# Feed-forward of a two-layer encoder trunk: the linear half scaled after w_down, more pairs by seven products

## The chip, the cores and the metric

The kernel runs on one core of one Trainium2 chip. The metric is the device time of one execution in microseconds (us): the median of the runs, and beside it the time and the span of one profiled execution. In rows of the profile, PE is the matmul engine (TensorE), PEld its weight loads, DVE is VectorE, ACT is ScalarE, POOL is GpSimd and SP the queue that issues most transfers.

## What is computed

Two layers over T = 528 tokens (16 meta tokens and 512 frames) of D = 1024. In each layer a mixer with two branches, and then a feed-forward with a short causal convolution on its gate; D_FF is 2816:

```python
def conv_gated_mlp(n, w_up, conv_w, w_down):
    gate, up = jnp.split(n @ w_up, 2, axis=-1)
    gate = causal_dwconv(gate, conv_w)          # three taps
    return (jax.nn.silu(gate) * up) @ w_down

    n = rms_norm(h, norm_ffn[l])
    h = h + conv_gated_mlp(n, w_up[l], conv_ffn[l], w_down[l])
```

`rms_norm` multiplies each token by a number of its own (`rb` in the kernel) and each feature by a gain. `rb` is the same for all features of a token, so it can be multiplied in on either side of a matmul that sums over features. On the way to `gate` it must stand ahead of silu; on `up`, which enters linearly, it can also stand behind `w_down`.

## The kernel before

Activations lie with features on the 128 partitions and tokens along the free axis. All operands are float32; each is split into a high and a low part (`wh`, `wl` of a weight tile, index 0 and 1 of an activation), and a product is three matmuls: high x high, high x low, low x high. A matmul takes 128 x 128 weights and up to 512 tokens into one PSUM bank. There are eight banks, two for each of the tags "a", "g", "s" and "x".

Weights come by `stage` (a load on SP into one of four `wst` buffers) and `two` (ScalarE copies the high part, VectorE subtracts for the low part, into one of three `wh` and three `wl` buffers). `tc.high_priority(HI)` puts these ahead of other work. A scheduler writes the order of each engine's queue when the kernel is built, by priority (program order otherwise) and by its own costs. On the chip each engine runs its queue in that order, and waits by semaphores.

In layer 0 all 528 tokens are worked on, in two halves of 264. In layer 1 only what is needed for the 512 frames: the gate in halves of about 257, the up half in one piece of 512 (one bank).

The feed-forward (`ffn`) first runs over FT = 22 columns j of the up-projection. A plain column has two calls of `dense` (the matmuls of L268): gate into tag "g" or "a", up into "s" or "a", for j even or odd. The gate is multiplied by `rb` into `cs` (L1133), convolved (L1136, L1138), and gated by tanh (L1140, L1141); the up half leaves its banks by a product with `rb` (L1148) and is multiplied by the gated half (L1149). For j in UP, gate and up come together from `up7`, by `seven` (matmuls at L284): a 2 x 2 block scheme with seven products for eight (the up half is then multiplied by `rb` at L1143), over pairs of k tiles, two output tiles and two token halves. Its banks are X1, X2 (tag "x"), two of tag "g" or "a", and `b2` of tag "s". The order in `seven` is: products into X1 and C0, then C2 (T4), then X2 and X1 (T2, T1), then C1 and X2 (B22, T3), with `steps` of additions between. Sums of weight blocks (L302 to L305) and of activation blocks are its operands; those for w_up are made after w_out in `layer`, in `xar` and `xq`. At j = 0, the statistics of the norm and the broadcast `rb` (`nf.stats`, `nf.rows`, L205 and L220 to L223) come among the matmuls: gate, statistics, the up half `pu0`, `rbp`, `rb`.

Then come four pairs m0 of output tiles of w_down. The last 2 x SP of the 22 k tiles go by `strassen` (`seven` over J0 to FT; its X1 is copied to P1 and combined to U2, U3, U4), the others by plain matmuls (`others`, L1245). For the first pair `strassen` stands ahead of the last piece of `others`, for the later ones ahead of all. Results are added to `hk`, which holds the residual stream (L1211, `addto`; L1263 where `wide`, that is, both halves in one bank, in layer 1 up to m0 = 4). After each pair of layer 0 the next norm is fed (`feed`: L187, L188, L194, L195); in layer 1 the tiles go to the output.

Of the kernel before, what the change touches and what calls it, by code (L numbers as in the profile page):

```python
# [10 lines left out]
F32 = mybir.dt.float32  # L11
# [16 lines left out]
SP = 4  # L28
INV = -2e38
UP = (2, 5, 8, 11, 14)  # L30
# [84 lines left out]
def _trunk(es, tc, nc, a):  # L115
# [162 lines left out]
    def seven(src, ks, ops, sums, X1, X2, C0, C1, C2, first, steps):  # L278
# [7 lines left out]

        def run(jobs, w, i, stride, off):

            for o, res, name, blk in jobs:
                for q in range(2):  # L290
                    mm3(o, first(res) if i == 0 and q == 0 else False, w, off * blk + stride * q, ops[2 * i + q][name])
# [6 lines left out]
        for i, r in enumerate(raw):  # L298
            t12, t34 = [t.rearrange("p (a q c) -> p a q c", a=2, q=2) for t in sums(i)]
            A = [r[i // 2][:, :, 128 * (i % 2):128 * (i % 2) + 128] for i in range(4)]  # L300
# [5 lines left out]
            ss.append([t.rearrange("p a q c -> p (a q c)") for t in (t12, t34)])  # L306
        n = range(len(ks))
        for i in n:
            run([(X1, "X1", "B11", 0), (C0, 0, "B21", 1)], wa[i], i, 256, 128)
        steps[0]()  # L310
        for i in n:
            w = [t.rearrange("p q c -> p (q c)") for t in two(raw[i][1][:, :, 128:], 256)]
            run([(C2, 2, "T4", 0)], w, i, 128, 0)
        for i in n:
            run([(X2, "X2", "T2", 1), (X1, "X1", "T1", 0)], two(ss[i][0], 512), i, 128, 256)
        steps[1]()
        for i in n:
            run([(C1, 1, "B22", 1), (X2, None, "T3", 0)], two(ss[i][1], 512), i, 128, 256)
# [6 lines left out]
    def layer(l, nm, before=None):  # L325
# [683 lines left out]
        for m in range(8):  # L1009
# [3 lines left out]
            if m % 2 == 0:  # L1013
                yt = Q((2, 3, 8, 9)[m // 2], [128, 2, 2, T], F32R, name="Y")
# [14 lines left out]
        xq = None  # L1029
        nf.ops = []  # L1030
        for m0 in range(0, 8, 2):
# [17 lines left out]
            if i == 3:  # L1049
                xq = Q(10, [128, 2112], F32R, name="xq")  # L1050
            tv = (xq if i == 3 else xar[:, 8 * nh * i:])[:, :8 * nh].rearrange("p (a b t) -> p a b t", a=4, b=2)
# [20 lines left out]
    def ffn(l, nf, h1, t0):  # L1072
# [11 lines left out]

        def up7(j, cs, uu):
# [23 lines left out]
            seven([a["w_up"][l, 2 * j + u] for u in range(2)], (0, 4), nf.ops,  # L1109
# [3 lines left out]
        for j in range(FT):  # L1113
            if j == J0:
                far = p1.tile([128, AR], F32R, tag="ar", name="far")
# [11 lines left out]
            if j in UP:  # L1127
                uu = p2.tile([128, T], F32, tag="hk", name="uu", bufs=2)
                up7(j, cs, uu)
                V.tensor_tensor(cs[:, 2 + t0:2 + T], cs[:, 2 + t0:2 + T], rb[:, t0:], op=mul)  # L1130
# [10 lines left out]
            V.scalar_tensor_tensor(cv[:, t0:], th[:, t0:], 1.0, cv[:, t0:], op0=add, op1=mul)  # L1141
            if j in UP:
                V.tensor_tensor(uu[:, t1:], uu[:, t1:], rb[:, t1:], op=mul)  # L1143
            else:
                ps = pu0 if j == 0 else dense(a["w_up"][l, 2 * j + 1], KT, lambda k, part: X[k][:, part], t1, "sa"[j % 2])
                uu = p2.tile([128, T], F32, tag="hk", name="uu", bufs=2)
                for p, t in ps:
                    V.tensor_tensor(uu[:, t], p, rb[:, t], op=mul)  # L1148
            V.tensor_tensor(uu[:, t1:], uu[:, t1:], cv[:, t1:], op=mul)  # L1149
            if j >= J0:  # L1150

                ys = yt[:, :8 * nh].rearrange("p (a b t) -> p a b t", a=4, b=2)
                ye = far[:, 6 * nh * ((j - J0) // 2):6 * nh * ((j - J0) // 2 + 1)].rearrange("p (a b t) -> p a b t", a=3, b=2)
# [12 lines left out]
                else:  # L1166
# [3 lines left out]
                    parts(ye[:, 0:2], halves(ue))  # L1170
                    V.tensor_tensor(uu[:, s1], uu[:, s1], ue[:, s1], op=sub)
                    parts(ye[:, 2:3], uu[:, None, s1])
                    S7.append(dict(B11=ys[:, 0], B21=ys[:, 1], B22=ys[:, 2], T1=ys[:, 3], T2=ye[:, 0], T3=ye[:, 1], T4=ye[:, 2]))
# [13 lines left out]
        for m0 in range(0, 8, 2):  # L1187
# [21 lines left out]
            def addto(i, x):  # L1209
                d = hks[i // 2][:, (s1, s2)[i % 2]]  # L1210
# [139 lines left out]
```

## Time and profile before

| what | value |
|---|---|
| median of 3 runs | 1697.04 us (1694.74 to 1697.94) |
| the profiled execution | 1696.78 us |
| its span, first to last instruction | 1695.0 us |
| granted TensorE clock, mean | 0.998 of full speed |
| TensorE busy | 1682.9 us, 99% |
| VectorE busy | 1360.1 us, 80% |
| ScalarE busy | 819.0 us, 48% |
| feed-forward of layer 0 (from the first gate matmul) | 479.64 to 858.45 us of the span |
| feed-forward of layer 1 | 1325.60 to 1691.60 us |

Matmuls are pipelined, so the duration of a record (some 284 ns for 264 columns) is not what one costs; the distance from start to start, or the length of a piece of the chain divided by its matmuls, is. Instructions on VectorE that follow each other without a wait overlap by some 0.08 us. Times in the rows count from the start of the span.

### The profile page before, as it was taken

The page shows a single profiled execution, that of the slowest core. Times are in us where ns is not written, and L with a number is a line of the kernel's source. Part 1 is how long each engine was busy: PE and PEld are TensorE (multiplying, and loading weights), DVE is VectorE, ACT ScalarE, POOL GpSimd, SP SyncE. Part 2 cuts the span into 40 slices and gives each one's busy share as a digit, 9 for nine tenths or more (in the row PEclk, how much of TensorE's full clock was granted, in tenths as well). Part 3 has the DMA queues.
Part 4 walks back from the last instruction along what each step waited for, and adds up shares of the span by engine and source line. Part 5 has one row for each costly group of instructions (what it writes and reads, how often), then busy time and mean ns, then how long its engine had stood idle before and what let it go on. Part 6 is the DMA issues. An engine that isn't in the chain of part 4 may idle for free.

```text
span 1695.0 us, 35229 instructions
## 1 busy us (share of the span) xinstructions
PE 1682.9 (99%) x13476; PEld 1579.7 (93%) x13476; DVE 1360.1 (80%) x3229; ACT 819.0 (48%) x1779; POOL 75.8 (4%) x190
## 2 busy tenths in 40 slices
PE   9999999999999999999999999999999999999999
PEld 8899988889999999999998999888899999999888
DVE  7899899866788888766558998998767888887754
ACT  6553556553444444434335534566635544444432
POOL 1000111100000000000100000110000000000000
PEclk9999999999999999999999999999999999999999
DMA  6322211225533333234433222112255433333443
GB/s 209 98 64 88 76 46 51 73 75 174 174 121 95 99 94 94 88 104 145 156 103 99 63 88 82 52 45 76 70 176 174 125 94 94 95 98 94 127 123 100
DMA packets 95097, 173.81 MB, mean 103 GB/s; under 512 B 10704, under 2 KB 15536, under 8 KB 94672
## 3 DMA queue, kind: packets, MB, share of 16 engines
q1 hardware_dynamic: 93456, 167.01, 32.5%
q10 hardware_dynamic: 1472, 4.54, 0.7%
q8 instruction: 106, 1.74, 0.4%
q14 instruction: 63, 0.52, 0.1%
HBM read 154.04 MB, written 17.06 MB: 101 GB/s over the span
## 4 chain that ended last, share of the span: by engine, by line
PE 90%; DVE 6%; ACT 3%; issue 1%; DMA 0%; ACTq 0%; DVEq 0%
PE a L268 55%; PE a L284 10%; PE a L1245 9%; PE misc L347 2%; PE iq L347 2%; PE vps L784 2%; PE oBT L947 1%; PE isc L530 1%; PE tps L795 1%; DVE wl L243 1%; PE logit L923 1%; PE PTp L941 1%; PE dS L838 1%; ACT ar L833 0%; ACT wh L242 0%
## 5 line engine op out<-in xcount | busy, mean ns | idle before, releaser
L268 PE MATMUL a<-X,wh 128*128 128x264 f32 (+4 forms) x4208 | 837.1, 295 | 0.6 <-DVE cs L1133 0.6
L268 PEld LDWEIGHTS a<-X,wh 128*128 128x128 f32 x4208 | 666.9, 189 | 17.7 <-issue 1.4
L268 PE MATMUL a<-X,wl 128*128 128x264 f32 (+4 forms) x2104 | 618.4, 294 | 0.0
L242 ACT ACTIVATE wh<-wst 128x512 fp32r<-128x512 f32 (+2 forms) x512 | 309.5, 605 | 537.7 <-PE a L268 284.6
L243 DVE TENSOR_TENSOR wl<-wst,wh 128x512 fp32r<-128x512 f32 (+2 forms) x512 | 335.8, 656 | 153.3 <-ACT wh L242 138.3
L268 PEld LDWEIGHTS a<-X,wl 128*128 128x128 f32 x2104 | 397.9, 189 | 9.1
L1245 PE MATMUL a<-F,wh 128*128 128x264 f32 (+2 forms) x728 | 154.8, 309 | 0.0
L1245 PEld LDWEIGHTS a<-F,wh 128*128 128x128 f32 x728 | 118.0, 188 | 7.3
L1245 PE MATMUL a<-F,wl 128*128 128x264 f32 (+2 forms) x364 | 112.7, 310 | 0.0
L268 PE MATMUL a<-Y,wh 128*128 128x264 f32 (+2 forms) x512 | 92.9, 283 | 0.0
L268 PEld LDWEIGHTS a<-Y,wh 128*128 128x128 f32 x512 | 79.1, 188 | 0.0
L268 PE MATMUL a<-Y,wl 128*128 128x264 f32 (+2 forms) x256 | 72.5, 283 | 0.0
L1245 PEld LDWEIGHTS a<-F,wl 128*128 128x128 f32 x364 | 68.6, 188 | 3.8
L1138 DVE SCALAR_TENSOR_TENSOR cv<-cs,vec,cv 128x528 f32<-128x528 f32 (+1 forms) x88 | 66.7, 758 | 2.7 <-ACT cv L1136 2.1
L405 DVE SCALAR_TENSOR_TENSOR cv<-cs,vec,cv 128x528 f32<-128x528 f32 x72 | 54.4, 758 | 0.9 <-ACT cv L403 0.8
L888 DVE MAX8 m<-ar 128x8 f32<-128x256 f32 (+2 forms) x96 | 53.2, 554 | 1.1
L889 DVE MATCH_REPLACE8 ar<-m,ar 128x256 f32<-128x256 f32 (+2 forms) x96 | 51.9, 541 | 0.0
L268 PEld LDWEIGHTS a<-Y,wl 128*128 128x128 f32 x256 | 48.2, 188 | 0.0
L284 PE MATMUL a<-F,wh 128*128 128x264 f32 (+1 forms) x256 | 47.9, 284 | 0.0
L284 PE MATMUL a<-xar,wh 128*128 128x264 f32 (+1 forms) x240 | 45.6, 283 | 0.0
L1140 ACT ACTIVATE th<-cv 128x528 f32<-128x528 f32 (+1 forms) x44 | 28.1, 638 | 35.7 <-DVE cv L1138 35.6
L284 PE MATMUL a<-X,wh 128*128 128x264 f32 (+1 forms) x240 | 44.8, 283 | 0.0
(401 smaller groups left out, 3057.1 us busy)
## 6 DMA issues: line engine op xcount, KB each, us to landing
wst<-w_up SPq DMA_DIRECT2D x176, 256.0 KB, 2.7
wst<-w_down SPq DMA_DIRECT2D x80, 256.0 KB, 2.7
wst<-w_a SPq DMA_DIRECT2D x64, 256.0 KB, 2.7
wst<-w_gate SPq DMA_DIRECT2D x64, 256.0 KB, 2.9
wst<-w_out SPq DMA_DIRECT2D x32, 256.0 KB, 2.9
hk<-h SPq DMA_DIRECT2D x24, 264.0 KB, 3.5
tg<-gg SPq DMA_DIRECT2D x16, 264.0 KB, 2.2
gr<-tg SPq DMA_DIRECT2D x16, 264.0 KB, 2.7
```

What stands on the lines that cost most here:

```text
L242: S.activation(h, w, AF.Copy)
L243: V.tensor_tensor(lo, w, h.bitcast(F32), op=sub)
L268: mms.append(PE.matmul(ps[j][:, :t.stop - t.start], w[:, ws], x[:, t], start=(kk == 0 and w is h and part == 0), stop=(kk == kts - 1 and w ...
L284: PE.matmul(o, ww[:, c:c + 128], x[:, part], start=st, stop=False, skip_group_check=True)
L347: mms.append(PE.matmul(b[:, c:], X[kk][:, part, o:o + 128], w[:, c:], start=(kk == 0 and w is h and part == 0), stop=(kk == KT - 1 and w i ...
L405: V.scalar_tensor_tensor(cv, cs[:, i:i + T], vc(cw + i), cv, op0=mul, op1=add)
L784: PE.matmul(p[r, ch], Ml[r, ch], U[r, ch], start=True, stop=True)
L888: V.max(m8, sc)
L889: V.match_replace(sc, m8, sc, SEL)
L1138: V.scalar_tensor_tensor(cv[:, t0:], cs[:, t0 + i:i + T], vec[:, cw + i:cw + i + 1], cv[:, t0:], op0=mul, op1=add)
L1140: S.activation(th[:, t0:], cv[:, t0:], AF.Tanh, scale=0.5)
L1245: PE.matmul(o, ww[:, 128 * k:128 * k + 128], Yf[k0 + k][:, part, t], start=first(2 * u + h) if k == 0 and part == 0 and ww is w[0] else False,
```

## The change

It has five parts.

1. UP has six columns, (1, 3, 6, 8, 10, 13), for five, (2, 5, 8, 11, 14).
2. SP is 5 for 4: ten of the 22 k tiles of w_down go by seven products, so `seven` takes groups of 2, 2 and 1 pairs instead of 2 and 2. It stages the third group's weights when the first two have been combined.
3. The up half is no longer multiplied by `rb`; it leaves its banks by a product with the gated half `cv`. Instead, the result of w_down is multiplied by `rb` before it is added to `hk`.
4. So the partial results `us` of `strassen` are no longer added to `hk` on their own: they are added to the banks C at the end of the pair, scaled, and added to `hk`. The last pair of layer 1 (`tail`) adds its scaled `us` earlier and scales each bank by itself.
5. Operands have other places: Y in buffers 2, 3, 5, 6 (2, 3, 8, 9 before), the sums for w_up in `ar`, 8 and 10, those for w_down in free parts of `ar` and, for the fifth pair, in the buffers of X6 and X7, and the third weight sum in the buffer of `ikT`.

The diff, cut to its core:

```diff
-SP = 4
+SP = 5
-UP = (2, 5, 8, 11, 14)
+UP = (1, 3, 6, 8, 10, 13)
...
         raw, ss, wa = [], [], []
-        for k in ks:
-            r = [stage(src[u][:, k * 128:k * 128 + 512], 512).rearrange("p (q c) -> p q c", q=2) for u in range(2)]
-            raw.append(r)
-            wa.append(two(r[0].rearrange("p q c -> p (q c)"), 512))
...
+        top = [load(i, 0) for i in range(2)]
+        raw = [[top[i], load(i, 1)] for i in range(2)]
         n = range(len(ks))
+        for i in range(2):
+            wa.append(two(raw[i][0].rearrange("p q c -> p (q c)"), 256 * np_[i]))
+        for i in n:
+            if i == 2:
+                raw.append([load(2, 0), load(2, 1)])
+                wa.append(two(raw[2][0].rearrange("p q c -> p (q c)"), 256 * np_[2]))
+            combine(i)
         for i in n:
             run([(X1, "X1", "B11", 0), (C0, 0, "B21", 1)], wa[i], i, 256, 128)
         steps[0]()
         for i in n:
-            w = [t.rearrange("p q c -> p (q c)") for t in two(raw[i][1][:, :, 128:], 256)]
+            w = [t.rearrange("p q c -> p (q c)") for t in two(raw[i][1][:, :, 128:], 128 * np_[i])]
             run([(C2, 2, "T4", 0)], w, i, 128, 0)
...
-                yt = Q((2, 3, 8, 9)[m // 2], [128, 2, 2, T], F32R, name="Y")
+                yt = Q((2, 3, 5, 6)[m // 2], [128, 2, 2, T], F32R, name="Y")
...
+            xt = xar[:, 2112 * i:] if i < 2 else Q((8, 10)[i - 2], [128, 2112], F32R, name="xq")
...
+        def extra(p):
+
+            v = lambda t, n: t[:, :2 * n * nh].rearrange("p (a b t) -> p a b t", a=n, b=2)
+            if p == 4:
+                x6, x7 = [p1.tile([128, 2 * T], F32R, tag=f"X{k}", name=f"FX{k}") for k in (6, 7)]
+                return v(x6, 2), v(x7, 1)
+            o, e = ((4224, 5280), (0, 1056), (1584, 2640), (3168, 5808))[p]
+            return v(far[:, o:], 2), v(far[:, e:], 1)
...
             if j in UP:
-                V.tensor_tensor(uu[:, t1:], uu[:, t1:], rb[:, t1:], op=mul)
+                V.tensor_tensor(uu[:, t1:], uu[:, t1:], cv[:, t1:], op=mul)
             else:
                 ps = pu0 if j == 0 else dense(a["w_up"][l, 2 * j + 1], KT, lambda k, part: X[k][:, part], t1, "sa"[j % 2])
                 uu = p2.tile([128, T], F32, tag="hk", name="uu", bufs=2)
                 for p, t in ps:
-                    V.tensor_tensor(uu[:, t], p, rb[:, t], op=mul)
-            V.tensor_tensor(uu[:, t1:], uu[:, t1:], cv[:, t1:], op=mul)
+                    V.tensor_tensor(uu[:, t], p, cv[:, t], op=mul)
...
                 def sums(i):
+                    if i == 2:
+                        t = p1.tile([128, 1024], F32, tag="ikT", name="s5")
+                        return t[:, :512], t[:, 512:]
...
             us = strassen()
+            tail = last and m0 == 6
             for i, k0 in enumerate(ks[n:]):
-                if i == 1 or m0 == 0:
-                    for c, x in enumerate(us):
-                        addto(c, x)
+                if tail and i == 1:
+                    for hk, w in zip(hks, us):
+                        V.tensor_tensor(w, w, rb[:, t1:], op=mul)
+                        V.scalar_tensor_tensor(hk[:, t1:], w, 0.5, hk[:, t1:], op0=mul, op1=add)
                 others(k0)
             for u in range(2):
-                hk, m = hks[u], m0 + u
-                if wide:
-                    V.scalar_tensor_tensor(hk[:, t1:], cb[u][:, :2 * nh], 0.5, hk[:, t1:], op0=mul, op1=add)
+                hk, m, w = hks[u], m0 + u, us[u]
+                if tail:
+                    for h, t in enumerate((s1, s2)):
+                        x = w[:, nh * h:nh * h + nh]
+                        V.tensor_tensor(x, C[2 * u + h], rb[:, t], op=mul)
+                        V.scalar_tensor_tensor(hk[:, t], x, 0.5, hk[:, t], op0=mul, op1=add)
                 else:
-                    for h in range(2):
-                        addto(2 * u + h, C[2 * u + h])
+                    if wide:
+                        V.tensor_tensor(w, w, cb[u][:, :2 * nh], op=add)
+                    else:
+                        for h in range(2):
+                            x = w[:, nh * h:nh * h + nh]
+                            V.tensor_tensor(x, x, C[2 * u + h], op=add)
+                    V.tensor_tensor(w, w, rb[:, t1:], op=mul)
+                    V.scalar_tensor_tensor(hk[:, t1:], w, 0.5, hk[:, t1:], op0=mul, op1=add)
```

## Rows read from the trace of the kernel before

**Rows 1.** The page, part 1: busy us of each engine, its share of the span, and the number of its instructions.

```profile
PE 1682.9 (99%) x13476; PEld 1579.7 (93%) x13476; DVE 1360.1 (80%) x3229; ACT 819.0 (48%) x1779; POOL 75.8 (4%) x190
```

**Rows 2.** Busy time in stretches of the span: first the length in us, then the busy us of each engine with its instructions, the granted clock, the share of the transfer engines and GB/s. The first stretch is three columns of the up-projection of layer 0 (two plain, one in UP), the others are the down-projections of layer 0 and 1.

```profile
515.94:549.68 33.74, 33.74 (x279) 33.74 (x278) 29.27 (x57) 15.93 (x27) 0.30 (x3) 1.00 0.32 95
733.10:858.45 125.35, 124.29 (x1010) 123.27 (x1010) 76.94 (x163) 46.53 (x86) 4.99 (x9) 1.00 0.44 133
1572.50:1691.60 119.10, 118.95 (x757) 107.19 (x755) 68.75 (x143) 38.76 (x69) 0.00 (x0) 1.00 0.40 117
```

**Rows 3.** The chain of waits in order of time, in both feed-forwards: start, length in us, what, and how many instructions were merged. L268 are plain products of w_up (192 of 264 columns are two columns j of layer 0; 72 are one of layer 1), L284 products in `seven`, L1245 plain products of w_down (264 columns at 733.10, 512 at 1642.05, 256 at 1671.62).

```profile
515.94 23.49 PE a L268 x192
...
539.43 10.24 PE a L284 x84
...
733.10 17.54 PE a L1245 x144
...
1339.34 11.34 PE a L268 x72
...
1383.88 10.09 PE a L284 x84
...
1632.02 10.02 PE a L284 x84
1642.05 19.56 PE a L1245 x84
...
1671.62 19.95 PE a L1245 x168
```

**Rows 4.** Groups of VectorE instructions in the first stretch of rows 2, shapes apart: line, operation, out<-in, shapes, count | busy us, mean ns of one | idle us before them, and who ended it.

```profile
L243 DVE TENSOR_TENSOR wl<-wst,wh 128x512 fp32r<-128x512 f32 x10 | 6.9, 687 | 1.1 <-ACT wh L242 1.1
L1138 DVE SCALAR_TENSOR_TENSOR cv<-cs,vec,cv 128x528 f32<-128x528 f32 x6 | 4.6, 762 | 0.0
...
L1149 DVE TENSOR_TENSOR uu<-uu,cv 128x528 f32<-128x528 f32 x3 | 2.1, 702 | 0.0
L1133 DVE TENSOR_TENSOR cs<-a,rb 128x264 f32<-128x264 f32 x4 | 1.7, 431 | 1.0 <-PE a L268 1.0
```

**Rows 5.** The timeline of TensorE in layer 1, in column j = 3, which follows a UP column: start, length, what, count and, in brackets, idle time before it and who ended it.

```profile
1366.26 0.28 PE L268 MATMUL a<-X,wl 128*128 128x258 f32 x1
1366.75 0.47 PE L268 MATMUL a<-X,wh 128*128 128x512 f32 x1 [0.22 <-DVE cs L1133]
```

**Rows 6.** The chain of waits at the same place.

```profile
1365.06 0.60 DVE uu L1143
...
1366.27 0.35 DVE cs L1133
```

**Rows 7.** The chain of waits at j = 0 of layer 0: the up half `pu0`, then `rbp`.

```profile
486.65 5.94 PE a L268 x48
492.59 1.11 PE rbp L220 x10
```

**Rows 8.** The timeline of ScalarE there.

```profile
493.51 0.51 ACT L222 ACTIVATE rb<-rbp 128x400 f32<-128x400 f32 x1 [0.34 <-PE rbp L220]
493.92 0.27 ACT L223 ACTIVATE rb<-rbp 128x128 f32<-128x128 f32 x1
496.02 0.74 ACT L1136 ACTIVATE cv<-cs,vec 128x528 f32<-128x528 f32 x1 [1.83 <-DVE cs L1133]
...
498.88 0.64 ACT L1140 ACTIVATE th<-cv 128x528 f32<-128x528 f32 x1 [1.60 <-DVE cv L1138]
```

**Rows 9.** The timeline of VectorE there; the first row is the two halves of `pu0` leaving their banks.

```profile
495.84 0.76 DVE L1148 TENSOR_TENSOR uu<-a,rb 128x264 f32<-128x264 f32 x2
496.80 0.77 DVE L1138 SCALAR_TENSOR_TENSOR cv<-cs,vec,cv 128x528 f32<-128x528 f32 x1 [0.19 <-ACT cv L1136]
...
498.08 0.76 DVE L1138 SCALAR_TENSOR_TENSOR cv<-cs,vec,cv 128x528 f32<-128x528 f32 x1
...
499.56 0.71 DVE L1141 SCALAR_TENSOR_TENSOR cv<-th,cv 128x528 f32<-128x528 f32 x1 [0.37 <-ACT th L1140]
```

**Rows 10.** The timeline of TensorE in layer 0, in `seven` of the third output pair of w_down, where the products of the first T2/T1 weight tile begin. Of the two matmuls in the first row the second starts at 800.07.

```profile
799.95 0.40 PE L284 MATMUL a<-far,wh 128*128 128x264 f32 x2
800.68 0.39 PE L284 MATMUL a<-far,wl 128*128 128x264 f32 x1 [0.33 <-DVE wl L243]
```

**Rows 11.** The timeline of ScalarE there: the feed of the next norm, the high part of that tile, and the copy of X1 to P1.

```profile
798.22 0.72 ACT L187 ACTIVATE X<-hk,gains 128x528 fp32r<-128x528 f32 x1
798.85 0.62 ACT L242 ACTIVATE wh<-s 128x512 fp32r<-128x512 f32 x1
...
800.95 0.36 ACT L1219 ACTIVATE ts<-a 128x264 f32<-128x264 f32 x1
```

**Rows 12.** The timeline of VectorE there: L195 reads the square that held a "th" buffer; the last row is three low parts of weight sums, one after the other.

```profile
798.64 0.70 DVE L195 TENSOR_TENSOR sqacc<-sqacc,sqt 128x528 f32<-128x528 f32 x1
799.26 0.76 DVE L188 SCALAR_TENSOR_TENSOR X<-hk,gains,X 128x528 fp32r<-128x528 f32 x1
799.94 1.91 DVE L243 TENSOR_TENSOR wl<-s,wh 128x512 fp32r<-128x512 f32 x3
```

**Rows 13.** The end of the chain of waits.

```profile
1688.96 2.62 PE a L1245 x22
...
1691.60 0.42 DVE hk L1211
```

**Rows 14.** The chain of waits just ahead of the hand-over of rows 10, on VectorE's side.

```profile
790.67 2.68 DMA wst<-w_down
```

More of the change, by code (lines that the diff above doesn't have):

```diff
@@ L285, in mm3, with load, combine @@
                 st = False
+        base, np_ = [0], []
+        for k, n in ks:
+            np_.append(n)
+            base.append(base[-1] + n)
         def run(jobs, w, i, stride, off):
             for o, res, name, blk in jobs:
-                for q in range(2):
-                    mm3(o, first(res) if i == 0 and q == 0 else False, w, off * blk + stride * q, ops[2 * i + q][name])
+                for q in range(np_[i]):
+                    mm3(o, first(res) if i == 0 and q == 0 else False, w, off * blk + stride * q, ops[base[i] + q][name])
         raw, ss, wa = [], [], []
-        for k in ks:
-            r = [stage(src[u][:, k * 128:k * 128 + 512], 512).rearrange("p (q c) -> p q c", q=2) for u in range(2)]
-            raw.append(r)
-            wa.append(two(r[0].rearrange("p q c -> p (q c)"), 512))
-        for i, r in enumerate(raw):
-            t12, t34 = [t.rearrange("p (a q c) -> p a q c", a=2, q=2) for t in sums(i)]
-            A = [r[i // 2][:, :, 128 * (i % 2):128 * (i % 2) + 128] for i in range(4)]
+        def load(i, u):
+            k, n = ks[i]
+            return stage(src[u][:, k * 128:k * 128 + 256 * n], 256 * n).rearrange("p (q c) -> p q c", q=n)
+        def combine(i):
+            r = raw[i]
+            t12, t34 = [t[:, :256 * np_[i]].rearrange("p (a q c) -> p a q c", a=2, q=np_[i]) for t in sums(i)]
+            A = [r[b // 2][:, :, 128 * (b % 2):128 * (b % 2) + 128] for b in range(4)]
             with tc.high_priority(HI):
@@ L1083, in ffn @@
         J0 = FT - 2 * SP
+        far = nf.ar
+        def extra(p):
[5 more added lines that the diff above has]
+            return v(far[:, o:], 2), v(far[:, e:], 1)
         def up7(j, cs, uu):
@@ L1107, in end @@
                 V.tensor_tensor(uu[:, z2], X1, U3, op=add)
-            seven([a["w_up"][l, 2 * j + u] for u in range(2)], (0, 4), nf.ops,
+            seven([a["w_up"][l, 2 * j + u] for u in range(2)], ((0, 2), (4, 2)), nf.ops,
                   lambda i: [sq[:, 1024 * i + 512 * u:1024 * i + 512 * u + 512] for u in range(2)],
@@ L1113, in ffn @@
         for j in range(FT):
-            if j == J0:
-                far = p1.tile([128, AR], F32R, tag="ar", name="far")
             if j % 2 == 0:
@@ L1169, in ffn @@
                     V.tensor_tensor(ue[:, s1], ue[:, s2], ue[:, s1], op=add)
-                    parts(ye[:, 0:2], halves(ue))
+                    ye, y4 = extra((j - J0) // 2)
+                    parts(ye, halves(ue))
                     V.tensor_tensor(uu[:, s1], uu[:, s1], ue[:, s1], op=sub)
-                    parts(ye[:, 2:3], uu[:, None, s1])
-                    S7.append(dict(B11=ys[:, 0], B21=ys[:, 1], B22=ys[:, 2], T1=ys[:, 3], T2=ye[:, 0], T3=ye[:, 1], T4=ye[:, 2]))
+                    parts(y4, uu[:, None, s1])
+                    S7.append(dict(B11=ys[:, 0], B21=ys[:, 1], B22=ys[:, 2], T1=ys[:, 3], T2=ye[:, 0], T3=ye[:, 1], T4=y4[:, 0]))
                 Yf.append(None)
@@ L1229, in sums @@
                 def sums(i):
+                    if i == 2:
+                        t = p1.tile([128, 1024], F32, tag="ikT", name="s5")
+                        return t[:, :512], t[:, 512:]
                     return (p2.tile([128, T + 3], F32, tag="cs", name="s12", bufs=2)[:, :512],
                             p2.tile([128, T], F32, tag="cv", name="s34", bufs=2)[:, :512])
-                seven(src, range(J0, FT, 4), S7, sums, X1, X2, C[0], C[1], C[2], first, (one, mid, end))
-                return P1, U4, U3, U2
+                seven(src, [(k, min(2, (FT - k) // 2)) for k in range(J0, FT, 4)], S7, sums, X1, X2, C[0], C[1], C[2], first, (one, mid, end))
+                return tt[:, :2 * nh], tu[:, :2 * nh]
             def others(k0):
```

18 lines of the change are left out of this document (6 added, 12 removed).

## The prediction

> **What bounds the kernel now.** I read the busy shares first: TensorE is busy for 1682.9 us of a span of 1695.0, VectorE for 1360.1, ScalarE for 819.0 [rows 1]. Busy TensorE says little here, since its ends are modelled, so I took the stretches of the feed-forward next [rows 2]: over three columns j of the up-projection TensorE has no gap in 33.74 us and VectorE works 29.27 of them; over the down-projection of layer 0 TensorE lacks 1.06 us of 125.35, over that of layer 1 0.15 of 119.10. Then the chain of waits in order of time [rows 3]: in both feed-forwards it is nearly all matmuls, at a steady pace. 84 matmuls of 264 columns take 10.24 us (121.9 ns each), 84 of 512 columns 19.56 us (232.9 ns), 84 of 256 columns 10.02 us (119.3 ns). So the feed-forward is bound by the number and width of matmuls. A matmul less is worth its pace, and anything that makes TensorE wait for a bank or a weight tile is paid in full.
>
> **The change, part by part.** The sum is made against the profiled execution, 1696.78 us; the median of the runs, 1697.04, lies 0.26 above it.
>
> *Matmuls of w_up.* UP grows from five to six columns in each layer. Layer 0: a column by two plain products takes 23.49 / 2 = 11.75 us, by seven products 10.24 [rows 3]: -1.50. Layer 1: 11.34 against 10.09: -1.25.
>
> *Matmuls of w_down.* Five pairs of k tiles instead of four. Layer 0: for each of four pairs of output tiles, 24 matmuls of 17.54 / 144 = 121.8 ns become 21: 4 x 3 x 0.122 = -1.46. Layer 1: the first three output pairs are `wide`, so 12 x 232.9 = 2.79 us become 21 x 119.3 = 2.51, -0.29 each; the last goes from 24 to 21 of about 119 ns (19.95 / 168 = 118.8): -0.35. Together -1.21. All matmuls: -5.42.
>
> The Trainium skill, "TensorE: Matmul & The Clock Gate", section "Wait — 56ns, not 53.3ns?", gives a warm matmul N / 2.4 GHz plus 2.5 ns, which is 112.5 ns for 264 columns and 215.8 for 512; the rows show 121.9 and 232.9, so the trace disagrees by some 8%. By the rule the matmuls would save an estimated 5.1 us; I keep the rows' figure.
>
> *VectorE, up-projection.* The linear half is no longer multiplied by `rb`. That takes one product of 512 or 528 elements off each of 44 columns, 0.70 us each [rows 4], some 0.62 in a back-to-back queue. It lies beside matmuls, except at one kind of place: in layer 1 the column after an even UP waits 0.37 us (the next matmul starts 0.49 after the last, whose pace is 0.12) for `cs` at L1133, since both its halves use bank tag "a" [rows 5], and one of the instructions ahead of that `cs` is the removed L1143, 0.60 us of the queue [rows 6]. Three even UP before (2, 8, 14), three after (6, 8, 10). 0.60 is more than 0.37: 3 x 0.37 = -1.1 (between 0, if VectorE is that much fuller, and -1.1).
>
> *A bank is held longer.* Now the up half leaves PSUM as `p * cv` instead of `p * rb`, so its bank is freed only after conv, tanh and gating. Where is that late? At j = 0 of layer 0. `pu0` takes both banks of tag "s" (two halves of 264), and the next column, j = 1, is now a UP, whose `b2` needs one. `rbp` ends at 492.59 + 1.11 = 493.70 [rows 7]. Then 24 matmuls into X1 and C0 follow, 2.93 us, to 496.6, and then C2 stands. `rb` is ready at 493.92 + 0.27 = 494.19 [rows 8]; from there two `cs` (0.76, as the pair of L1148), the copy 0.74, two L1138 (1.45), tanh 0.64, L1141 0.71, half a product 0.43 [rows 8, 9], with some 0.3 of hand-offs: 499.2. TensorE stands 2.7 us, or 1.2 if the 12 matmuls of T2 and T1 are put into the hole. In the trace the same chain took to 499.56 + 0.71 = 500.27, with weight tiles between; then 4.1. I take 2.0. In layer 1 `pu0` needs one bank (512 columns), the other is free: 0. At j = 3 and 13 of layer 0 the up matmuls (5.86 us) and the first 24 (2.93) cover the chain of some 6.5: 0; with the eight sums (8 x 0.34) ahead of it 0.4 each, for the range.
>
> *Three steps in `seven`.* With five pairs the stages are 2 + 2 + 1 pairs. A tag of three weight buffers lets the first T2/T1 tile be made only when the tile three before it is used up: before, 12 matmuls (1.46 us) ahead of its need; now 6 + 3 = 9 (1.10). Making it takes 0.62 on ScalarE and 0.69 on VectorE. That is short already: at 800.07 the third matmul of this tile waits 0.49 [rows 10], behind the feed of the next norm [rows 11, 12]. So 0.36 more at three hand-overs of layer 0, +1.1; layer 1 has no feed there and some 0.4 spare, so +0.3 over its four. Together +1.4 (0 to 8 x 0.36 = 2.9). The number of weight DMAs stays at 12 for each output pair; the third step's two loads on SP wait for buffers of the first.
>
> *The end of an output pair.* The `us` were added to `hk` during the next plain matmuls; now four additions, two products by `rb` and two updates of 528 stand behind the last matmul. Against four updates before that is 2 x 0.62 + 2 x 0.69 = 2.6 us more of VectorE, at the place where the next pair's `seven` wants it. What waits: banks of C, which six rotating banks cover; `hk` for the next pair, not wanted until that pair's end; and the "th" buffers that hold `us`, one of which becomes the next P1. P1 was copied at 800.95 [rows 11], though its buffer was free from 798.64 + 0.70 = 799.34 [rows 12]: 1.6 of slack. 1.1 is missing, and nine T2 matmuls (1.1 us) can stand in: 0 to 3 x 1.1; I take +0.4. The hand-over to layer 1's projection frees a bank of tag "g" up to 0.8 later, with other banks to go on with: +0.2.
>
> *The last store.* After the last matmul one update of 0.42 [rows 13] becomes a product and an update: +0.4.
>
> *Operands' places.* Y, xq, far and FX6/FX7 move to buffers whose readers end earlier; no instruction is added. FX6 and FX7 wait for the last matmul of column 21, as does `uu` itself: 0.
>
> Sum: -5.42 - 1.1 + 2.0 + 1.4 + 0.4 + 0.2 + 0.4 = -2.1, which gives 1694.7.
>
> **The rivals.**
>
> *All covered.* The order written into the queues fills the hole at j = 0 and the tiles are made in time, as almost everywhere in [rows 3]: -5.42 - 1.1 + 0.4 = -6.1, 1690.7. Against it: the waits of [rows 5, 10], which show that the covers are thin. Chance 0.27.
>
> *VectorE becomes the bound of the up-projection.* Columns 6 to 10 alternate now; before, two plain columns followed each UP. Two columns: TensorE 21.99 us; VectorE 29.27 less three products (1.9) less a plain column (some 6.7) = 20.7, 94%. Should the queue not overlap instructions, it counts by durations [rows 4]: about 22.5, 0.5 too much, for three such stretches in each layer +3.0: 1697.7. The Trainium skill, "Trainium Kernel Development and Optimization", section "Best Practices", says to mind PSUM pressure, since "TensorE tiling speeds up compute but not PSUM evacuation"; seven products save matmuls and not evacuations, which is this rival, and [rows 2], with 4.47 us of VectorE free in three columns, do not bear it out so far. Chance 0.10.
>
> *Slower: the P1 buffer comes late.* VectorE takes its instructions in the order of its queue, and sums of high priority stand ahead of the end-of-pair work. Before, the queue stood 2.68 us behind one load of w_down [rows 14]. The third step's loads wait for buffers in just this place. If that wait now holds back the update that frees "th", X1 stays full, and TensorE stands about 2.7 us at each of three hand-overs of layer 0: +8.0, 1702.7. It decides from 1.9 each, where 1700.4 is passed. Against it: before, TensorE did not stand for that load. Chance 0.09.
>
> *It does nothing measurable,* the waits of j = 0 and `seven` at their upper bounds eating it: 1696 to 1697.5. Chance 0.06, beside the forecast's 0.48.
>
> **How the numbers follow.** About 0.2% (3.4 us) is what a measurement of this kernel tells from no change, so faster means under 1693.6. The likeliest case, 0.48, has its own range of 1692.5 to 1697, about a quarter of it under 1693.6: 0.11. With "all covered" 0.27 that is 0.38. Slower: 0.09 and a little of the VectorE case, 0.10. The rest, 0.52. Range: 1690.3 (all covered) to 1699.8 (VectorE bound with the upper bounds of the waits).
>
> **What would show it.** Column times of 10.24 and 10.09 us at six UP; 105 matmuls of `seven` in 12.8 us at each pair of layer 0; no wait for L1133's successor in layer 1; a hole of 1 to 3 us some 3 us after `rbp` of layer 0, ended by the product of `uu`; and a wait of about 0.85 for the first T2 weight tile at the hand-overs. A hole over 4 us at j = 0, gaps ended by P1's copy, or VectorE full in columns 6 to 10 would make it wrong.

## The result, and the profile after

The changed kernel is slower: 1708.68 us (median of 6 runs, 1707.25 to 1709.69) against 1697.18 of the kernel before beside it, a ratio of 1.0070 with an interval of 1.0057 to 1.0083. The forecast was 1694.7, in a range of 1690.3 to 1699.8. The profiled execution took 1708.53 us, its span 1706.7, at a granted clock of 0.999.

The page of the changed kernel answers to [rows 1]: the busy shares tell nothing of 12 us.

```profile
PE 1684.4 (99%) x13488; PEld 1577.2 (92%) x13488; DVE 1372.3 (80%) x3286; ACT 826.2 (48%) x1811; POOL 75.5 (4%) x190
```

So the stages come first. The table gives their lengths, each from the first matmul of the stage to the first of the next (w_down to the start of its own last matmul), and what the sum of the prediction makes of them.

| stage | before | forecast | after | after less forecast |
|---|---|---|---|---|
| columns j, layer 0 | 253.3 | 253.8 | 260.5 | +6.7 |
| w_down, layer 0 | 125.2 | 125.2 | 126.3 | +1.1 |
| columns j, layer 1 | 246.7 | 244.3 | 250.9 | +6.6 |
| w_down, layer 1 | 118.9 | 118.0 | 118.7 | +0.7 |

Nearly nine tenths of the surplus lie in the columns. TensorE's longest waits there, of the whole execution (engine, tile and line, what it waited for and its line: us in total, times, longest):

```profile
PE a L284 <- ACT wh L242: 6.4, 10, 0.7
PE a L284 <- DVE wl L243: 3.1, 8, 0.8
...
PE a L284 <- ACT ts L1240: 1.3, 1, 1.3
```

Weight tiles of `seven`, then, for which the kernel before waited 1.0 us in all (the third row, the copy of X1 to P1, belongs to w_down). The chain of layer 0 shows one of the places, behind the gate of column 7 (start, us, what):

```profile
560.51 0.64 ACT wh L242
...
563.80 3.21 DMA wst<-w_up
...
567.03 0.42 DVE wsum L309
...
571.92 0.61 DVE wl L243
...
572.58 1.00 PE a L284 x6
573.58 5.85 PE a L268 x48
```

What TensorE, ScalarE and VectorE did there, in their timelines (start, us; last the idle time before and what ended it):

```profile
567.65 0.28 PE L268 MATMUL a<-X,wl 128*128 128x264 f32 x1
568.58 0.75 PE L284 MATMUL a<-X,wh 128*128 128x264 f32 x4 [0.65 <-ACT wh L242]
569.73 0.39 PE L284 MATMUL a<-X,wl 128*128 128x264 f32 x1 [0.40 <-DVE wl L243]
...
571.63 0.76 PE L284 MATMUL a<-X,wh 128*128 128x264 f32 x4 [0.65 <-ACT wh L242]
572.58 0.39 PE L284 MATMUL a<-X,wl 128*128 128x264 f32 x1 [0.19 <-DVE wl L243]
...
573.42 0.41 PE L268 MATMUL a<-X,wh 128*128 128x264 f32 x2
```

```profile
561.97 0.63 ACT L242 ACTIVATE wh<-wst 128x512 fp32r<-128x512 f32 x1 [0.82 <-PE a L284]
...
565.23 0.63 ACT L242 ACTIVATE wh<-wst 128x512 fp32r<-128x512 f32 x1 [1.24 <-PE a L268]
...
567.90 0.63 ACT L242 ACTIVATE wh<-wst 128x512 fp32r<-128x512 f32 x1 [1.29 <-PE a L268]
...
570.95 0.63 ACT L242 ACTIVATE wh<-wst 128x512 fp32r<-128x512 f32 x1
```

```profile
567.03 0.42 DVE L309 TENSOR_TENSOR wsum<-wst 128x256 f32<-128x256 f32 x1 [0.44 <-DMA wst<-w_up]
...
571.23 0.70 DVE L1202 TENSOR_TENSOR F<-uu,F 128x528 fp32r<-128x528 f32 x1
571.84 0.68 DVE L243 TENSOR_TENSOR wl<-wst,wh 128x512 fp32r<-128x512 f32 x1
572.45 0.41 DVE L312 TENSOR_TENSOR wsum<-wst,wsum 128x256 f32<-128x256 f32 x1
572.78 0.76 DVE L1158 TENSOR_TENSOR cs<-a,rb 128x264 f32<-128x264 f32 x2
```

The gate of column 7 has its last matmul at 567.65. Its up half (L268) should follow, but TensorE's queue has the first stage of column 8 (L284, X1 and C0) ahead of it: the up half of an odd column needs the banks of tag "a" that the gate still holds, and the gate leaves them only at 572.78 (L1158), behind the rest of column 6 and the weight sums of column 8, which have high priority and themselves waited 0.44 for a load. With that exit the up half could not have started before 573.2, whatever TensorE's queue has next. And column 8's stage, put into the hole, runs at about half its pace. It starts behind the tile that ScalarE makes at 567.90 and goes on behind that of 570.95. The two ahead of these, of 561.97 and 565.23, must then be the up half's two tiles, since the up half starts at 573.42 with no tile made in between (the next follows at 576.58); passed by, they hold two of three buffers, and column 8's second tile has to wait until its first is used up. From 567.65 to 573.42 are 5.77 us for 25 matmuls that take 3.05 at the pace of 0.122: 2.7 lost. With nothing in the hole it would have been some 5.4 (573.2 less 567.8, an estimate); so the loss comes from the gate's late exit, and the stage that passes hides a part of it. The same stands behind the gate of column 9 in layer 0 (2.3 above pace), and behind 7 and 9 in layer 1 (2.3 and 2.6). These four places are 9.9 of the 13.3 us by which the columns exceed the forecast.

Over 25 us VectorE is not full there. These two windows hold the two places of layer 0 (busy us of PE, PEld, DVE, ACT, POOL):

```profile
565.00:590.00 25.00, 23.11 (x181) 22.19 (x181) 20.45 (x42) 10.90 (x19) 0.20 (x2) 1.00 0.27 86
590.00:615.00 25.00, 23.51 (x186) 22.61 (x185) 20.77 (x43) 11.28 (x20) 0.20 (x2) 1.00 0.28 90
```

But in the stretch just ahead of the gate's exit it is busy for 11.11 us of 11.58, so what stands first in its queue there decides what comes late:

```profile
561.20:572.78 11.58, 9.69 (x73) 8.85 (x72) 11.11 (x23) 4.53 (x7) 0.10 (x1) 1.00 0.38 116
```

The three theories that followed: A, the order of the queues and the banks of tag "a"; B, VectorE as the bound where columns alternate; C, the loss lies elsewhere, in w_down and the scaling.

### The profile page after: what moved, and what is told of

Same layout as the page of the kernel before. It is cut to its first block, busy times and chain, and to the rows that moved or that the text cites. A ratio compares the mean times of both kernels' runs of the same rounds, so it can differ in the third digit from the quotient of the medians.

```text
span 1706.7 us, 35385 instructions
## 1 busy us (share of the span) xinstructions
PE 1684.4 (99%) x13488; PEld 1577.2 (92%) x13488; DVE 1372.3 (80%) x3286; ACT 826.2 (48%) x1811; POOL 75.5 (4%) x190
## 4 chain that ended last, share of the span: by engine, by line
PE 88%; DVE 8%; ACT 3%; issue 1%; DMA 1%; ACTq 0%; DVEq 0%
PE a L268 53%; PE a L284 11%; PE a L1269 7%; PE misc L364 2%; PE iq L364 2%; DVE wl L243 1%; PE vps L801 1%; PE oBT L964 1%; PE isc L547 1%; PE tps L812 1%; PE logit L940 1%; PE PTp L958 1%; ACT wh L242 1%; DMA wst<-w_up 1%; PE dS L855 0%
## 5 line engine op out<-in xcount | busy, mean ns | idle before, releaser
L268 PE MATMUL a<-X,wh 128*128 128x264 f32 (+3 forms) x4096 | 812.9, 295 | 0.0
L268 PEld LDWEIGHTS a<-X,wh 128*128 128x128 f32 x4096 | 647.9, 189 | 15.8 <-issue 0.2
L268 PE MATMUL a<-X,wl 128*128 128x264 f32 (+4 forms) x2048 | 600.9, 293 | 0.0
L242 ACT ACTIVATE wh<-wst 128x512 fp32r<-128x512 f32 (+3 forms) x512 | 307.2, 601 | 543.3 <-PE a L268 284.6
L243 DVE TENSOR_TENSOR wl<-wst,wh 128x512 fp32r<-128x512 f32 (+3 forms) x512 | 333.1, 652 | 142.3 <-ACT wh L242 125.5
L268 PEld LDWEIGHTS a<-X,wl 128*128 128x128 f32 x2048 | 386.7, 189 | 8.7
L1269 PE MATMUL a<-F,wh 128*128 128x264 f32 (+2 forms) x624 | 132.6, 309 | 0.0
L1269 PEld LDWEIGHTS a<-F,wh 128*128 128x128 f32 x624 | 101.2, 188 | 6.2
L268 PE MATMUL a<-Y,wh 128*128 128x264 f32 (+2 forms) x512 | 92.8, 283 | 0.0
L268 PEld LDWEIGHTS a<-Y,wh 128*128 128x128 f32 x512 | 79.0, 188 | 0.0
L284 PE MATMUL a<-xar,wh 128*128 128x264 f32 (+2 forms) x384 | 73.8, 285 | 1.5 <-ACT wh L242 1.3
L268 PE MATMUL a<-Y,wl 128*128 128x264 f32 (+2 forms) x256 | 72.4, 283 | 0.0
L284 PEld LDWEIGHTS a<-xar,wh 128*128 128x128 f32 x384 | 59.2, 188 | 2.4 <-ACT wh L242 1.7
L284 PE MATMUL a<-F,wh 128*128 128x264 f32 (+1 forms) x320 | 60.0, 283 | 1.3 <-ACT ts L1240 1.3
L284 PE MATMUL a<-X,wh 128*128 128x264 f32 (+1 forms) x288 | 55.2, 287 | 5.1 <-ACT wh L242 5.1
L284 PE MATMUL a<-xar,wl 128*128 128x264 f32 (+2 forms) x192 | 56.0, 293 | 1.2 <-DVE wl L243 0.9
```

What stands on the lines that cost most here:

```text
L242: S.activation(h, w, AF.Copy)
L243: V.tensor_tensor(lo, w, h.bitcast(F32), op=sub)
L268: mms.append(PE.matmul(ps[j][:, :t.stop - t.start], w[:, ws], x[:, t], start=(kk == 0 and w is h and part == 0), stop=(kk == kts - 1 and w ...
L284: PE.matmul(o, ww[:, c:c + 128], x[:, part], start=st, stop=False, skip_group_check=True)
L1269: PE.matmul(o, ww[:, 128 * k:128 * k + 128], Yf[k0 + k][:, part, t], start=first(2 * u + h) if k == 0 and part == 0 and ww is w[0] else False,
```

## The experiments

Each is timed against the kernel before, on the same chip; the ratio has its 95% interval.

**The gate's exit first (cs_first).**

```diff
-                for p, t in ps:
-                    V.tensor_tensor(cs[...], p, rb[:, t], op=mul)
+                with tc.high_priority(HI if j in (7, 9) else 0):
+                    for p, t in ps:
+                        V.tensor_tensor(cs[...], p, rb[:, t], op=mul)
```

> The changed kernel, in which the product that takes the gate of columns 7 and 9 out of its banks (cs<-a,rb) has the high priority that weight tiles and weight sums have; UP stays (1, 3, 6, 8, 10, 13). A: the banks of tag a come free before the sums of the next UP column, the up half is not passed by that column's first stage, and the four places shrink: 1698 to 1701. B: VectorE has the same work, so 1708.7, or more since the sums come later. C: 1708.7.

1696.64 us, 1.0005 (0.9996 to 1.0014): 0.65% less than the changed kernel, or 11 us, which brings it back to the kernel before and not under it. Not an instruction was added or taken away. In its chain, the stretch that held the hole is matmuls at pace (11.75 us for 96, 10.24 for 84, as the forecast took them from [rows 3]):

```profile
554.98 8.65 PE a L284 x71
563.63 11.75 PE a L268 x96
575.38 10.24 PE a L284 x84
```

and the gate's two halves leave among the sums (L1159 here):

```profile
568.08 0.43 DVE L1159 TENSOR_TENSOR cs<-a,rb 128x264 f32<-128x264 f32 x1
...
570.05 0.43 DVE L1159 TENSOR_TENSOR cs<-a,rb 128x264 f32<-128x264 f32 x1
```

VectorE is fuller in this stretch than ahead of the late exit (11.71 us of 11.75), and TensorE has no gap in it:

```profile
563.63:575.38 11.75, 11.75 (x99) 11.75 (x98) 11.71 (x26) 5.25 (x9) 0.10 (x1) 1.00 0.35 110
```

VectorE is full either way, so what decides is the order in its queue: B falls, and C for the larger part. The columns take 254.9 us in layer 0 and 245.1 in layer 1 now, for 260.5 and 250.9.

**Other columns (up_apart, up_odd, up_old).**

```diff
-UP = (1, 3, 6, 8, 10, 13)
+UP = (1, 3, 6, 9, 12, 15)  # up_apart
+UP = (1, 3, 5, 7, 9, 13)  # up_odd
+UP = (2, 5, 8, 11, 14)  # up_old
```

> The changed kernel with UP = (1, 3, 6, 9, 12, 15): still six columns, but no plain odd column stands between two even UP columns. Theory A (order): in the changed kernel a plain odd column between two even UP columns (7 and 9) has gate and up half both in the two banks of tag a; the gate leaves late, the queue runs the first stage of the next UP column ahead of the up half, against weight tiles that are not ready; four such places of 2.5 to 3 us. They vanish: 1708.7 - 11 = 1697.7, within 1. Theory B (VectorE is full where UP and plain columns alternate): two of three alternating stretches go, 1708.7 - 7 = 1701.5. Theory C (the loss lies in w_down and in the scaling, not in the columns' pattern): 1708.7.

1698.23, 1.0014 (1.0005 to 1.0023).

> The changed kernel with UP = (1, 3, 5, 7, 9, 13): six columns, four alternations, but the plain columns between are even, whose gate and up half have tags of their own (g and s). A: the four places of 2.5 to 3 us vanish (-11), and three more plain even columns of layer 0 hold both s banks ahead of a UP column, as at j = 2 now, 1.4 each (+4): about 1702. B: one alternating stretch more than now, so not faster: 1708.7 to 1712. C: 1708.7.

1702.48, 1.0041 (1.0028 to 1.0053).

> The changed kernel with the old UP = (2, 5, 8, 11, 14); all the rest of the change stays. A: the four places (-11), the hole at j = 0 (-1.5) and the wait at j = 2 (-1.4) go, one column less by seven products in each layer costs 1.50 + 1.25: 1697.6. B: the same within 1. C: 1708.7 + 2.75 = 1711.5.

1701.95, 1.0039 (1.0026 to 1.0051).

The first two are within 0.6 of A, and up_odd, with more alternations and less time, speaks against B. The third misses A by 4.4. Its trace has a passed up half again, behind the gate of column 1 in both layers, where column 2 is next (0.81, 0.38 and 0.76 us above pace in layer 0, 0.81, 0.30 and 0.76 in layer 1), and w_down of layer 0 takes 127.3, 2.1 more than before and 1.0 more than in the changed kernel; together some 4.8 us, about the 4.4. So a place needs no UP column on both sides: a plain odd column ahead of an even one is enough, where VectorE is late. The kernel before, with the same UP, has such columns too (1, 7 and 13) and no passed up half; up_old has none at 7 and 13.

**The scaling of the linear half (scaled_before, rb_only).** Both take part 3 of the change back; scaled_before keeps the gate's priority of cs_first, rb_only does not.

```diff
             if j in UP:
-                V.tensor_tensor(uu[:, t1:], uu[:, t1:], cv[:, t1:], op=mul)
+                V.tensor_tensor(uu[:, t1:], uu[:, t1:], rb[:, t1:], op=mul)
...
-                    V.tensor_tensor(uu[:, t], p, cv[:, t], op=mul)
+                    V.tensor_tensor(uu[:, t], p, rb[:, t], op=mul)
+            V.tensor_tensor(uu[:, t1:], uu[:, t1:], cv[:, t1:], op=mul)
...
-                    V.tensor_tensor(w, w, rb[:, t1:], op=mul)
```

The products by `rb` in the last pair of layer 1 go too.

> cs_first with the linear half multiplied by rb as before the change (the up half leaves its banks by p*rb and is then multiplied by cv; no product by rb behind w_down). All else stays, the additions of us to the banks C too. If the later exit of the up half and the two products at each pair's end cost more than VectorE gains by 44 products less: the hole at j = 0 (1.5), the wait at j = 2 (1.2) and the wait for P1 at the second pair of layer 0 (1.5) go: 1696.6 - 4 = 1692.5. If the relief of VectorE is what makes the six columns possible: 1699 or more.

1691.33, 0.9970 (0.9959 to 0.9982): faster than both kernels.

> The changed kernel with the linear half scaled as before the change (p*rb, then times cv; no rb behind w_down), and no priority given to any gate: scaled_before (1691.3) without its high priority for the gates of 7 and 9. If alternating columns alone make the gate late and let the next UP column's first stage pass the up half: the four places remain, 1691.3 + 11 = 1702. If the later exit of the up half (p*cv) is what makes it late: no such place, 1691 to 1692. Halfway values would mean that both are needed in some of the four.

1700.15, 1.0025 (1.0014 to 1.0035): near the first value. The two places of layer 0 shrink to 0.8 us each, those of layer 1 stay at 2.5 and 2.2; another 2.2 are one wait for a weight tile in w_down of layer 0, which scaled_before does not have. So the order makes the places, and the later exit lengthens those of layer 0. Against cs_first, scaled_before wins 2.7 in the columns of layer 0 (254.9 to 252.2: the hole at j = 0 and the wait at j = 2) and 2.9 in w_down of layer 0. The relief of VectorE by 44 products, which the change was costed for, is worth less than its two consequences, at these six columns.

**Four pairs in w_down again (cs_first_sp4, rb_sp4).** Both have SP = 4 for 5, in cs_first and in scaled_before.

> cs_first (1696.6) with SP = 4 as before the change: four pairs of w_down by seven products, in two steps of seven. Gives up 1.46 + 1.21 = 2.7 us of matmuls. Theory T (the third step costs what it saves: beyond before, TensorE stands 2.5 us more in w_down of layer 0 and 1.1 in that of layer 1): 1696.6 + 2.7 - 3.6 = 1695.7. Theory E (those waits come from the arithmetic at the end of an output pair, which SP = 4 keeps): 1696.6 + 2.7 - 0.5 = 1698.8.

1711.21, 1.0085 (1.0071 to 1.0099). Neither theory: w_down of layer 0 takes 137.9 us. The wait that grew is that for P1's copy, three times in layer 0 and once in layer 1:

```profile
PE a L284 <- ACT ts L1241: 10.4, 4, 3.7
```

ScalarE's timeline at the second pair of layer 0 shows why it is late:

```profile
773.37 0.74 ACT L187 ACTIVATE X<-hk,gains 128x528 fp32r<-128x528 f32 x1 [1.38 <-DVE hk L1302]
774.01 0.63 ACT L191 ACTIVATE sqacc<-hk 128x528 f32<-128x528 f32 x1
775.75 0.73 ACT L187 ACTIVATE X<-hk,gains 128x528 fp32r<-128x528 f32 x1 [1.11 <-DVE hk L1302]
776.39 0.63 ACT L194 ACTIVATE sqt<-hk 128x528 f32<-128x528 f32 x1
776.92 0.37 ACT L1241 ACTIVATE ts<-a 128x264 f32<-128x264 f32 x1
```

The copy stands in ScalarE's queue behind the feed of the second output tile, which waits for the last update of `hk`. X1 was complete by 773.35, where TensorE came to a stop. That is the prediction's third rival, but in layer 0 by way of ScalarE's queue. At the one place in layer 1 there is no feed, and the copy waits for an update of `hk` itself. These updates are what reads `us` last, and `us` lies in the "th" buffers, so this is the rival as it was put:

```profile
1622.45 0.38 ACT L1241 ACTIVATE ts<-a 128x256 f32<-128x256 f32 x1 [3.13 <-DVE hk L1302]
```

The waits cost more than their length. Behind the first and the third of them, after TensorE stood 3.7 and 2.7 us, its granted clock is 0.50 for a while, the lower of its two levels (1.2 of 2.4 GHz), and a matmul of 264 columns takes 0.22 us instead of 0.122: some 4 us in all. Behind the second, of 2.7 too, the clock stays at 1.00. One of the two stretches:

```profile
778.00:780.60 2.60, 2.60 (x13) 2.60 (x13) 1.54 (x3) 1.22 (x2) 0.00 (x0) 0.50 0.50 153
```

> cs_first_sp4 (1711.2, of which TensorE stood 10.4 us for P1's copy) with the linear half scaled as before: no product by rb behind w_down; the additions of us to the banks C stay. If the two products by rb at a pair's end are what makes the copy late: 1691.3 (scaled_before, SP = 5) + 2.7 = 1694. If moving the additions of us to the pair's end is enough for it: 1702 to 1705.

1700.10, 1.0023 (1.0014 to 1.0032): between the two. The same wait is

```profile
PE a L284 <- ACT ts L1242: 4.8, 3, 2.5
```

so some 5.6 of the 10.4 come from the products by `rb`, and 4.8 from what stays: presumably the additions moved to the pair's end, but the loads and sums of `seven` have another order too, and the two were not taken apart. One stretch at the lower clock is left, worth some 1.5 us. With SP = 5 the third step lays 12 more matmuls (1.5 us) between the start of a pair's `seven` and the need for P1; in scaled_before no wait for P1 is left. How much of that is the order that the queues then have was not taken apart. SP = 5 is worth 9 us there, for 2.7 of matmuls; the wait for P1 and the clock behind it make the rest, 4.8 and 1.5.

**The pair's end (end_first, even7b_tail).** end_first puts the additions, the product and the update at high priority.

> cs_first with the arithmetic at the end of an output pair of w_down (additions of C, product by rb, update of hk) at high priority, so ahead of the next pair's weight tiles. Theory E: the wait of 1.5 for P1 in layer 0 goes, whose copy stood in ScalarE's queue behind the feed that waits for hk: 1695.0. Theory T: unchanged or worse, since the first T2 tiles come later: 1697 to 1699.

1699.60, 1.0017 (1.0008 to 1.0026). The wait for P1 is gone, but the first weight tiles of the next pair now come late, 2.2 us above pace at the second pair of layer 0 and 2.4 at that of layer 1, with some 1.6 more at the lower clock behind the latter: the wait has moved, and the sum is worse.

even7b_tail, on a kernel described next, ends every pair as the last one is ended; where both halves lie in one bank, one product and one update do for them:

```diff
-            tail = last and m0 == 6
+            tail = True
...
-                if tail and i == 1:
+                if i == 1 or m0 == 0:
```

> even7b (1691.1) in which every output pair of w_down is ended as the last one is: us is scaled and added to hk during the following plain matmuls, and behind the last matmul stand only the products of the banks C by rb and the updates of hk (two instructions less per output tile where both halves lie in one bank, one less of 528 where they do not). If the length of the pair's end is what makes P1 and the weight tiles late: w_down of layer 0 stands 4.8 us now and about 2.2 then, 1688.5. If VectorE's total or the third step of seven is what counts: 1691 or more.

1692.40, 0.9977 (0.9969 to 0.9986): no gain, and the wait for P1, at the same single place, has grown from 1.3 to

```profile
PE a L284 <- ACT ts L1241: 3.1, 1, 3.1
```

So it is not the number of instructions behind the last matmul that sets this wait, but what stands ahead of the copy when it is due: in the trace of even7b_tail the feeds of both output tiles (767.81 to 771.00) stand ahead of it, in even7b one of the two was done by 763.8. Why the order came out so was not isolated.

**More columns (even7, even7b, rb_even7, rb_mix8).**

```diff
-UP = (1, 3, 6, 8, 10, 13)
+UP = (2, 4, 6, 8, 10, 12, 14)  # even7, even7b, rb_even7
+UP = (1, 3, 5, 7, 9, 11, 13, 15)  # rb_mix8
...
+                with tc.high_priority(HI if j - 1 in UP and j + 1 in UP else 0):  # even7
+                with tc.high_priority(HI if j + 1 in UP else 0):  # the others
```

> The changed kernel with seven columns, UP = (2, 4, 6, 8, 10, 12, 14), and the product that takes a gate out of its banks (cs<-a,rb) at high priority in every plain column between two UP columns. Theory A (order): one column more by seven products, -2.75; no UP at j = 1, so no hole (-1.6), and no plain even column between UP columns, so no wait at j = 2 (-1.4), against cs_first at 1696.6: 1690.9. Theory B (VectorE is full where columns alternate): seven alternations in a row leave it no recovery, 1697 or more.

1696.48, 1.0003 (0.9994 to 1.0012).

> even7 (1696.5) with priority for the gate of column 1 too, which stands ahead of a UP column and was passed in both layers of even7 (0.81, 0.39 and 0.76 us in layer 0, 0.81, 0.30 and 0.76 in layer 1): 1696.5 - 3.8 = 1692.7. If the passing is no cause of those waits: 1696.5.

1691.07, 0.9972 (0.9962 to 0.9981). The clearest test of A: even7 missed it because column 1, with a UP column only behind it, had no priority; giving it that takes 0.31% off, 5.3 us. The columns take 250.1 and 243.9 us; no other set of columns takes less.

> scaled_before with seven columns, UP = (2, 4, 6, 8, 10, 12, 14), and priority for the gate of every plain column ahead of a UP column (column 1 too). If order is all: one column more, 1691.3 - 2.75 = 1688.6. If VectorE is full once it has its 44 products back and seven alternations: 1694 or more.

1691.48, 0.9973 (0.9962 to 0.9983).

> scaled_before with eight columns, UP = (1, 3, 5, 7, 9, 11, 13, 15). Plain columns between are even, with gate and up half in tags of their own. If order and banks are all: two columns more, 1691.3 - 5.5 = 1685.8. If VectorE is the bound at eight alternations with its 44 products back: 1692 or more.

1691.94, 0.9975 (0.9966 to 0.9984). Neither gets what its added columns save: rb_even7 loses the 2.75 of one, rb_mix8 the 5.5 of two. Here theory B has a share. A window over columns of layer 0 in even7b and then in rb_even7, which has the 44 products (busy us of PE, PEld, DVE, ACT, POOL, as above):

```profile
490.00:725.00 235.00, 235.00 (x1926) 234.95 (x1925) 202.00 (x403) 114.77 (x198) 1.98 (x20) 1.00 0.31 94
```

```profile
490.00:725.00 235.00, 234.26 (x1910) 233.31 (x1909) 212.70 (x422) 113.96 (x196) 1.98 (x20) 1.00 0.31 93
```

At 86% of VectorE TensorE has no gap, at 91% it has some, of 0.8 us and less, behind weight tiles and gates. The mean hides where: the largest, 0.81 behind a tile at 654.37, lies in a stretch where VectorE is busy for 14.94 us of 15 in rb_even7 and 14.38 in even7b, in the columns from 12 on, whose results are also split and combined for `strassen`:

```profile
640.00:655.00 15.00, 14.63 (x118) 14.21 (x116) 14.94 (x33) 8.92 (x16) 0.10 (x1) 1.00 0.33 98
```

rb_mix8 loses some 4 us of its 6 in the same part of layer 0: TensorE stands 1.81 us for a weight tile at 653.92, behind VectorE, which works without a pause from 643.11 on, and then runs some matmuls at the lower clock. Part 3 thus pays in the columns once seven of them alternate and the gates go first (even7b's are 1.9 and 2.5 us shorter than rb_even7's), and costs 2.8 of that back in w_down of layer 0. In all, the two kernels are not told apart (0.9972 and 0.9973).

## Why the prediction was wrong, step by step

- *Matmuls, -5.42: right.* 10.24 us for 84 matmuls in a column (cs_first, above); in w_down of layer 0 the 105 of `seven` take 13.08, 124.6 ns each with small waits, where [rows 3] gave 121.8:

```profile
739.44 11.69 PE a L1269 x96
751.13 13.08 PE a L284 x105
764.21 5.84 PE a L1269 x48
```

  With the order mended and the scaling put back, scaled_before comes out 0.30% or 5.1 us under the kernel before, close to this term; 4.3 of the 5.1 lie in the four stages of the table, and gains and small waits of other terms are among them.
- *VectorE in the up-projection, -1.1: this step failed.* It took VectorE's work to lie beside matmuls except at one place, the column behind an even UP in layer 1 [rows 5, 6], and put at nothing what the new columns do to the order in VectorE's queue. That was the right place with the wrong question. The 0.37 came from a plain odd column whose gate leaves bank "a" late. The change put two such columns, in both layers, right ahead of another UP column, whose sums of high priority make the gate later still. The waits of [rows 5] should have been read as "how late can the gate be before TensorE runs out of work that it may do", and not as a number that 0.60 less of queue takes away. The four places took 9.9 us where 1.1 were to be won, and giving the gate its place in the queue (cs_first) was worth 11.
- *The rival "VectorE becomes the bound" named the right columns (6 to 10)*, at +3.0, and for a wrong reason: over 25 us VectorE is busy for 82% and 83% there, and in the stretch where it is full cs_first has it fuller and loses nothing. At the ends of rb_even7 and rb_mix8 its mechanism does show. The Trainium skill's warning about PSUM evacuation ("Trainium Kernel Development and Optimization", section "Best Practices") fits this case in a narrower sense than I gave it: evacuation was late by its place in the queue, for the banks of one tag.
- *The hole at j = 0, +2.0: right in size, in part by luck.* Only 0.33 above pace, behind 498.42, is ended by the product of `uu` as foretold. 0.82, behind 495.77, is a wait for the first T2 tile, the stage that the order put into the hole, which the working had taken to run. About 1.5 in all:

```profile
495.77 0.29 PE L284 MATMUL a<-X,wl 128*128 128x264 f32 x1
496.72 0.75 PE L284 MATMUL a<-xar,wh 128*128 128x264 f32 x4 [0.66 <-ACT wh L242]
...
498.87 0.51 PE L284 MATMUL a<-xar,wh 128*128 128x264 f32 x2 [0.17 <-DVE uu L1174]
```

- *j = 2 ahead of j = 3, 0 with 0.4 for the range: too small.* The same wait for a T2 tile as at j = 0 stands behind 519.36, about 1.3 in all:

```profile
520.30 0.76 PE L284 MATMUL a<-xar,wh 128*128 128x264 f32 x4 [0.66 <-ACT wh L242]
```

- *Three steps in `seven`, +1.4: near in size, and half of the story.* Without its matmuls and the 1.5 us for P1, w_down is 1.1 us longer than before in layer 0 and 0.9 in layer 1, in waits of some tenths (at the third and fourth pair of layer 0 that of [rows 10] is 0.53, for 0.48 before); that holds small waits of other terms too. But with two steps instead the kernel is 9 to 14 us slower (rb_sp4, cs_first_sp4), since the third step covers P1. The working looked at what the third step makes late and not at what it gives time to.
- *The end of an output pair, +0.4, and the rival "the P1 buffer comes late", +8.0 at 0.09: the mechanism was real and came once.* It cost 1.5 us above pace at the second pair of layer 0. At SP = 4 it costs 10.4 and the clock behind it. (The missing slack was 2.6 less 1.6, 1.0 and not 1.1.) I priced the "th" buffer [rows 11, 12], but in this kernel the copy waits in ScalarE's queue behind the feed of `hk`, which the longer end delays:

```profile
777.12 0.70 DVE L1301 SCALAR_TENSOR_TENSOR hk<-tu,hk 128x528 f32<-128x528 f32 x1
```

```profile
777.86 0.73 ACT L187 ACTIVATE X<-hk,gains 128x528 fp32r<-128x528 f32 x1 [1.40 <-DVE hk L1301]
...
779.03 0.37 ACT L1240 ACTIVATE ts<-a 128x264 f32<-128x264 f32 x1
```

- *The last store, +0.4: right*; a product and an update stand behind the last matmul for the update of [rows 13]:

```profile
1702.74 0.42 DVE L1291 TENSOR_TENSOR tu<-a,rb 128x256 f32<-128x256 f32 x1 [0.54 <-PE a L1269]
1703.20 0.42 DVE L1292 SCALAR_TENSOR_TENSOR hk<-tu,hk 128x256 f32<-128x256 f32 x1
```

- *Operands' places, 0: no wait seen that names them.* They were not tried apart.

What stays open: why the wait for P1 stands at the second pair alone with SP = 5, how much of rb_sp4's wait for P1 each of the remaining parts makes, and what the order written into the queues, which every edit changes, adds to a difference of one or two us.

## What to carry to other kernels

Where queues are written ahead, a late exit from a bank does not cost just its lateness: work that was put into the gap may hide a part of it, and may itself fail for want of weight buffers that the blocked work holds. For each bank ask what must leave it, what of higher priority stands ahead of that in the engine's queue, and which stage is next in TensorE's queue if it is late; here a priority on two gates, without one instruction less, was worth 11 us. A change that relieves one engine by holding a bank or ending a stage later is to be costed by the moment that the held thing is wanted, not by the instructions saved; and a short copy that frees a bank should not stand behind a feed of the next stage on its engine. An engine's busy share over a long stretch tells neither: here 82% over 25 us held 11.6 us in which VectorE was full.
